# A DiT block with 32 experts on one core: the experts' weights loaded in pieces of 2 MB instead of 1 MB

## The chip, the core and the metric

The kernel runs on one core of one Trainium2 chip. The metric is the device time of one execution in microseconds (us). The core has a matrix engine (TensorE, PE in the profile; PEld is its weight load), a vector engine (DVE), a scalar engine (ACT), GpSimd (POOL) and a sync engine (SP) that here only issues transfers. Sixteen DMA engines move the data between the memory outside (HBM) and the on-chip memory, which has 128 partitions.

## What is computed

One transformer block over 256 tokens of width 1024: modulation from a condition vector, two kinds of attention (global, and windowed with a sink), a gated merge, and then a mixture of 32 experts of which each token uses four. The part that matters here is the mixture; everything is float32.

```python
def moe(h, w_router, b_router, w_e1, b_e1, w_e2, b_e2):
    t = h.reshape(-1, shape[-1])                      # 256 x 1024
    top_logit, top_idx = lax.top_k(t @ w_router + b_router, TOP_K)
    combine = ...                                     # 256 x 32, four weights in a row
    for e in range(N_EXPERTS):                        # 32
        u = t @ w_e1[e] + b_e1[e]                     # w_e1[e]: 1024 x 2048, 8 MB
        u_glu = jnp.minimum(u[:, 0::2], SWIGLU_LIMIT)
        u_lin = jnp.clip(u[:, 1::2], -SWIGLU_LIMIT, SWIGLU_LIMIT)
        act = u_glu * jax.nn.sigmoid(SWIGLU_ALPHA * u_glu) * (u_lin + 1)
        out = out + combine[:, e:e + 1] * (act @ w_e2[e] + b_e2[e])   # w_e2[e]: 1024 x 1024, 4 MB
```

## The kernel before

**The weights' stream.** All large weights pass through areas of 16 KB on each partition (2 MB in all): seven that exist from the start (`ring0` to `ring6`), and two more, `xx` and `ptt`, which the attention uses first and which `grow` hands over when it is done. Each area counts as two halves of 8 KB. The list `pieces` holds every load in order: the modulation's and the projections' weights, `w_br`, `w_o`, and then the experts. `pump` walks it: it takes the oldest free half, issues the piece's transfer on SP (line 111) and stops where no half is free. `done` gives a half back after the last matmul that reads it, and calls `pump`. SP issues strictly in this order; a transfer waits on SP for the engines that last read its half, and for one of eight semaphores that the transfers use in turn (so at most eight of SP's transfers are under way).

**The experts' pieces.** `w1[e, k]` (k = 0 to 7) is one 1 MB piece, 128 rows of the input dimension by 2048 columns; `w2[e, k]` (k = 0 to 3) is 1 MB too, two blocks of 128 rows by 1024. On each partition a piece is one row of 8 KB. The order is: all of w1(0), and then for each e: w1(e+1, 0 and 1), w2(e, 0 to 3), w1(e+1, 2 to 7). The last expert (31) is loaded in halves of its columns: each of its pieces is two transfers of 512 KB whose rows on a partition are pairs of 2 KB (lines 99 and 105).

**The engines' order.** The text of the kernel is the order. Each expert handles up to 64 gathered tokens. For each e: `scatter` adds an earlier pair's result, `bias1(e+1)` starts the sums, `gemm1` (line 835) runs k = 0 of expert e+1, `act_turn(e)` turns expert e's activations, `gemm1` runs k = 1, `gemm2(e)` (line 871) reads the four w2 pieces, `gemm1` runs k = 2 to 7, and `act(e+1)` follows on DVE and ACT. Between two k's there stands now and then a `gather` (line 805) or a `spread` (line 822). A k of `gemm1` is eight PE instructions, a `gemm2` is 32. After expert 30's `gemm1` comes the end: `half1` (line 970) and `half2` (line 1107) of expert 31, with a branch on a register in between (line 1017, a path for overfull experts that isn't taken here).

Of the kernel before, what the change touches and what calls it, by code (L numbers as in the profile page):

```python
# [17 lines left out]
NE = 32  # L18
# [16 lines left out]
def tile_dit_block(ctx: ExitStack, tc: tile.TileContext, xcT, consts, small, rows,  # L35
                   w_m0, w_q, w_mod, w_in, w_br, w_o, w_r, w1, b1, w2, b2, out):
    nc = tc.nc
# [6 lines left out]
    pieces = []  # L44
# [7 lines left out]
    def w1s(e, ks):  # L52
        pieces.extend(("w1", (e, k), w1[e, k]) for k in ks)

    def w2s(e):
        pieces.extend(("w2", (e, k), w2[e, k]) for k in range(4))

    for j in range(10):
        if j < 8:
# [6 lines left out]
    ins(7), mods(10, 11), ins(8), mods(12, 13), ins(9), mods(14, 15)  # L66
    pieces.extend(("br", i, w_br[i]) for i in range(4))
    pieces.extend(("wo", i, w_o[i]) for i in range(4))
    w1s(0, range(8))
    for e in range(NE - 1):  # L70
        w1s(e + 1, range(2))
        w2s(e)
        w1s(e + 1, range(2, 8))
    w2s(NE - 1)


    areas = [per.tile([128, 4096], F32, name=f"ring{i}") for i in range(N_PAIR)]
    spare = [(i, h) for i in range(N_PAIR) for h in range(2)]
    n_next = [0]
    held, place = {}, {}  # L80

    def half(a):
        return areas[a[0]][:, 2048 * a[1]:2048 * a[1] + 2048]

    def pump():
        while n_next[0] < len(pieces):
            kind, idx, src = pieces[n_next[0]]
            if kind == "xc":
                nc.sync.dma_start(out=xc, in_=xcT[1])
                n_next[0] += 1  # L90
                continue
            if not spare:
                return
            place[kind, idx] = spare.pop(0)
            t = held[kind, idx] = half(place[kind, idx])
            if kind == "w2" and idx[0] == NE - 1:
                h, q = divmod(idx[1], 2)
                for b in range(2):
                    nc.sync.dma_start(
                        out=t[:, 1024 * b:1024 * b + 1024].rearrange("p (k c) -> p k c", k=2),  # L100
                        in_=w2[NE - 1, q + 2 * b].rearrange("p (k c) -> p k c", k=2)[:, :, 512 * h:512 * h + 512])
            elif kind == "w1" and idx[0] == NE - 1:
                h, q = divmod(idx[1], 4)
                for b in range(2):
                    nc.sync.dma_start(
                        out=t[:, 1024 * b:1024 * b + 1024].rearrange("p (a c) -> p a c", a=2),
                        in_=w1[NE - 1, 2 * q + b].rearrange("p (a h c) -> p a h c", a=2, h=2)[:, :, h, :])
            elif kind == "q":
                nc.sync.dma_start(out=t[:, 0:1024], in_=src)
            else:  # L110
                nc.sync.dma_start(out=t, in_=src)
            n_next[0] += 1

    def take(kind, idx):
        return held[kind, idx]

    def done(kind, idx):
        held.pop((kind, idx))
        spare.append(place.pop((kind, idx)))
        pump()  # L120

    def grow(t):

        areas.append(t)
        spare.extend((len(areas) - 1, h) for h in range(2))
        pump()
# [153 lines left out]
    for j in range(8):  # L280
# [15 lines left out]
        if j > 4:  # L296
            i, k = ((0, 1), (2, 3), (0, 2))[j - 5]
# [396 lines left out]
    for m in range(8):  # L694
        w = take("wo", m // 2)[:, 1024 * (m % 2):1024 * (m % 2) + 1024].rearrange("p (k c) -> p k c", k=8)
# [133 lines left out]
    def gemm1(e, u, ks, between=None):  # L829
        p, j = divmod(e, 2)  # L830
        for k in ks:
            w = take("w1", (e, k))
            for ch in (0, 2, 1, 3):
                c0 = 64 * (ch // 2)
                nc.tensor.matmul(u[c0:c0 + 64, ch % 2, :], XT[p][:, k, 64 * j:64 * j + 64],  # L835
                                 w[:, 512 * ch:512 * ch + 512], start=False, stop=(k == 7))
            done("w1", (e, k))
            if between and k in between:
                between[k]()

# [13 lines left out]
    def act_turn(e, aT=None):  # L854
        t = TMP.pop(e)
        tp = ps2.tile([128, 4, 128], F32, name="ta", tag="tp")
        for b in range(4):
            nc.tensor.transpose(tp[:, b, :], t[:, 0, 128 * b:128 * b + 128], ident)  # L858
        if aT is None:
            aT = t[:, 3, :].rearrange("p (b s) -> p b s", b=4)  # L860
        nc.scalar.copy(out=aT, in_=tp)  # L861
        return aT

    def gemm2(e, aT, between=None):
        p, j = divmod(e, 2)
        y = ps2.tile([128, 512], F32, name="y", tag="y")
        for k in range(8):
            w = take("w2", (e, k // 2)).rearrange("p (k c) -> p k c", k=2)[:, k % 2, :]
            l = aT[:, k % 4, 64 * (k // 4):64 * (k // 4) + 64]
            for h in range(2):  # L870
                nc.tensor.matmul(y[64 * h:64 * h + 64, :], l, w[:, 512 * h:512 * h + 512],  # L871
                                 start=(k == 0), stop=(k == 7))
            if k % 2:
                done("w2", (e, k // 2))
                if between and k // 2 in between:
                    between[k // 2]()
        if e >= NE - 2:
            YY[e] = x_t[:, 0, 512 * (e % 2):512 * (e % 2) + 512]
            nc.vector.tensor_tensor(out=YY[e], in0=y, in1=g2x, op=ALU.mult)
            return  # L880
        if j == 0:
            YY[p] = y_t[0][:, p % 2, :]
        for h in range(2):
            nc.vector.tensor_tensor(out=YY[p][64 * j:64 * j + 64, 512 * h:512 * h + 512],  # L884
                                    in0=y[64 * h:64 * h + 64, :],
                                    in1=g2[64 * h:64 * h + 64, 512 * h:512 * h + 512], op=ALU.mult)
# [63 lines left out]
    for e in range(NE - 2):  # L950
        p, j = divmod(e, 2)
# [4 lines left out]
        aT = act_turn(e)  # L956
# [5 lines left out]
    e0, e1 = NE - 2, NE - 1  # L962
    sums = {}

    def half1(h, q, u):
        w = take("w1", (e1, 4 * h + q)).rearrange("p (b a c) -> p b a c", b=2, a=2)
        for b in range(2):
            k = 2 * q + b
            for i in range(2):
                nc.tensor.matmul(u[64 * i:64 * i + 64, h, :], XT[e1 // 2][:, k, 64:128], w[:, b, i, :],  # L970
                                 start=False, stop=(k == 7))
        done("w1", (e1, 4 * h + q))

    def act_half(h, u):
        t, c = tmp4, slice(256 * h, 256 * h + 256)
# [23 lines left out]
    aT = act_turn(e0)  # L999
# [17 lines left out]
    with tc.If(cnt > CAP):  # L1017
# [20 lines left out]
        def body(e):  # L1038
            ws = []
            for k in range(8):  # L1040
                w = slots[k]
                nc.sync.dma_start(out=w, in_=w1[bass.ds(e, 1), k].rearrange("e p n -> (e p) n"))
                ws.append(w)
            cv = moe.tile([128, 2], F32, name="cv")
            for tb in range(2):
# [4 lines left out]
            for tb in range(2):  # L1050
                aT = y_t[0][:, tb, :].rearrange("p (k s) -> p k s", k=8)
                for ch in range(4):
# [4 lines left out]
                    t = tmp4  # L1057
                    ub, a = t[:, 0, :], t[:, 1, :]
# [13 lines left out]
            vs = []  # L1072
            for k in range(4):
                w = slots[k]
                nc.sync.dma_start(out=w, in_=w2[bass.ds(e, 1), k].rearrange("e p n -> (e p) n"))
                vs.append(w.rearrange("p (k c) -> p k c", k=2))
            for tb in range(2):
                aT = y_t[0][:, tb, :].rearrange("p (k s) -> p k s", k=8)
                for h in range(2):
                    s = slice(512 * h, 512 * h + 512)  # L1080
# [3 lines left out]
                    t = per.tile([128, 512], F32, name="bt", tag="msb")  # L1084
# [14 lines left out]
    aT = tmp4[:, 3, :].rearrange("p (b s) -> p b s", b=4)  # L1099
    yl = [ps2.tile([128, 512], F32, name="yl", tag="y")]  # L1100

    def half2(h, q):
        w = take("w2", (e1, 2 * h + q)).rearrange("p (k c) -> p k c", k=4)
# [11 lines left out]
    for h in range(2):  # L1115
        s = slice(512 * h, 512 * h + 512)
# [4 lines left out]
        for tb in range(2):  # L1121
            a = ACC[0][:, tb, s]
# [10 lines left out]
    for tb in range(2):  # L1133
# [5 lines left out]
        for h in (1, 0):  # L1139
            s = slice(512 * h, 512 * h + 512)  # L1140
# [25 lines left out]
def _pack(a):  # L1166
    import numpy as np
    f = lambda n: np.asarray(a[n])
    h = np.arange(64)
# [12 lines left out]
    rows[0, 0:8] = f("sink")[0]  # L1182
    rows[0, 32:64] = f("b_router")[0]
    rows[0, 1024:2048] = f("final_g")
    pair = lambda w: np.ascontiguousarray(
        w.reshape(w.shape[:-2] + (w.shape[-2] // 256, 2, 128, w.shape[-1])).swapaxes(-3, -2)
    ).reshape(w.shape[:-2] + (w.shape[-2] // 256, 128, 2 * w.shape[-1]))
    tT = lambda t: np.ascontiguousarray(t.T.reshape(8, 128, 256).transpose(1, 0, 2))
    con = np.ascontiguousarray

# [18 lines left out]
                    .reshape(2, 4, 128, 4, 256).transpose(3, 2, 0, 1, 4)).reshape(4, 128, 2048),  # L1209
        "w_o": con(f("w_o")[0].reshape(8, 128, 4, 2, 128).transpose(2, 1, 3, 0, 4)).reshape(4, 128, 2048),  # L1210
        "w_r": con(f("w_router")[0].reshape(8, 128, 32).transpose(1, 0, 2)),
        "w1": con(f("w_e1")[0].reshape(32, 1024, 4, 256, 2).swapaxes(-1, -2)).reshape(32, 8, 128, 2048),
        "b1": con(f("b_e1")[0].reshape(32, 4, 256, 2).swapaxes(-1, -2)).reshape(128, 512),
        "w2": pair(f("w_e2")[0]),
        "b2": be2,
    }

# [17 lines left out]
```

## Time and profile before

| | us |
|---|---|
| median of 3 runs | 1224.25 (1223.93 to 1226.63) |
| profiled execution, its own time | 1224.82 |
| its span, first to last instruction | 1223.0 |
| PE busy in the span | 1159.1 |
| bytes on SP's and ACT's hardware queues | 454.06 MB + 2.06 MB |

The profile gives for each engine the busy time, and cuts the span into 40 slices of 30.6 us. Matmuls are pipelined and their ends are modelled: a PE that is shown as busy is not a PE at its peak. The front, up to some 275 us, holds the modulation, the attention and the routing; the experts run from there to 1191 us, and the rest is the end of expert 31 and the output.

### The profile page before, as it was taken

The numbers are of one execution on the slowest core, as the hardware profiler recorded it, in microseconds if no ns is written. First come the engines' busy times: TensorE is split into PE (matmuls) and PEld (weight loads), VectorE is DVE, ScalarE is ACT, GpSimd is POOL, SyncE is SP. The second block draws the span as 40 slices with busy tenths as digits, with TensorE's granted clock in tenths as the row PEclk, the third lists the DMA queues.
The fourth block names the chain that finished last, engine by engine and source line by source line (L and its number), as shares of the span: only waits on it lengthen the run. The fifth ranks groups of instructions, "written<-read, shape, count | busy, mean of one in ns | idle before, by whom it ended". The sixth has DMA issues, their size and how long they took to land. (4 is left out here: it accounts for less than half of the span.)

```text
span 1223.0 us, 13639 instructions
## 1 busy us (share of the span) xinstructions
PE 1159.1 (95%) x5624; PEld 529.7 (43%) x5624; DVE 359.1 (29%) x765; ACT 138.8 (11%) x304; POOL 35.2 (3%) x29
## 2 busy tenths in 40 slices
PE   7999999999999999999999999999999899999987
PEld 5888666883343334343434323232323232323222
DVE  3263665332222242322222222222222222222212
ACT  2122553030000000000000000000000000000002
POOL 0231100000000000000000000000000000000000
PEclk9999999999999999999999999999999999999997
DMA  9976655838999999999999999999999999999992
GB/s 379 377 296 212 235 206 201 342 134 361 422 421 421 421 420 421 421 421 421 421 421 422 421 421 421 421 421 421 421 421 421 420 421 421 421 421 421 414 391 75
DMA packets 70066, 458.36 MB, mean 375 GB/s; under 512 B 7848, under 2 KB 8240, under 8 KB 16752
## 3 DMA queue, kind: packets, MB, share of 16 engines
q1 hardware_dynamic: 68304, 454.06, 90.9%
q10 hardware_dynamic: 1296, 2.06, 0.5%
q0 software_dynamic: 400, 1.32, 0.3%
q8 instruction: 46, 0.75, 0.2%
q14 instruction: 20, 0.16, 0.0%
HBM read 456.36 MB, written 1.05 MB: 374 GB/s over the span
## 5 line engine op out<-in xcount | busy, mean ns | idle before, releaser
L835 PE MATMUL u<-ring,t 128*64 128x512 f32 x1488 | 346.0, 600 | 21.7 <-DMA ring<-w 21.7
L835 PEld LDWEIGHTS u<-ring,t 128*64 128x64 f32 x1488 | 99.5, 137 | 223.8 <-issue 162.9
L871 PE MATMUL y<-ring,r_q 128*64 128x512 f32 x832 | 184.2, 593 | 0.0
L884 DVE TENSOR_TENSOR t<-y,r_kv 64x512 f32<-64x512 f32 x60 | 41.3, 689 | 325.6 <-PE y L871 325.2
L871 PEld LDWEIGHTS y<-ring,r_q 128*64 128x64 f32 x832 | 59.3, 137 | 119.6 <-issue 115.8
L845 DVE TENSOR_SCALAR r_q<-u 128x512 f32<-128x512 f32 x31 | 21.4, 692 | 244.0 <-PE u L835 244.0
L835 PE MATMUL u<-ptt,t 128*64 128x512 f32 x320 | 75.6, 598 | 4.4 <-DMA ptt<-w 4.4
L847 ACT ACTIVATE r_q<-r_q 128x512 f32<-128x512 f32 x31 | 19.5, 630 | 505.8 <-DVE r_q L845 505.8
L688 PE MATMUL u<-mtx,keep 128*64 128x512 f32 x256 | 62.2, 604 | 3.0 <-DVE r_q L848 3.0
L805 PEld LDWEIGHTS xg<-mtx,r_y 128*128 128x128 f32 x512 | 58.4, 192 | 12.2 <-issue 12.2
L805 PE MATMUL xg<-mtx,r_y 128*128 128x128 f32 x512 | 61.3, 278 | 0.0
L368 PE MATMUL mm<-xx,ring 128*128 128x256 f32 x256 | 59.9, 385 | 0.0
L894 PE MATMUL sp<-t,mtx 128*128 128x512 f32 x120 | 59.7, 620 | 0.0
L368 PEld LDWEIGHTS mm<-xx,ring 128*128 128x128 f32 x256 | 47.3, 190 | 12.6 <-issue 5.0
L807 DVE TENSOR_TENSOR t<-xg,modb 128x512 f32<-128x512 f32 x32 | 22.1, 692 | 91.1 <-PE xg L805 91.1
L835 PE MATMUL u<-xx,t 128*64 128x512 f32 x176 | 40.4, 596 | 3.7 <-DMA xx<-w 3.7
L835 PEld LDWEIGHTS u<-ptt,t 128*64 128x64 f32 x320 | 21.6, 136 | 48.3 <-issue 34.4
L895 DVE TENSOR_TENSOR r_t<-r_t,sp 128x512 f32<-128x512 f32 x60 | 38.4, 681 | 5.1 <-PE sp L894 5.1
L894 PEld LDWEIGHTS sp<-t,mtx 128*128 128x128 f32 x120 | 20.5, 191 | 39.5 <-issue 39.5
L871 PE MATMUL y<-xx,r_q 128*64 128x512 f32 x160 | 36.3, 594 | 0.0
L688 PEld LDWEIGHTS u<-mtx,keep 128*64 128x64 f32 x256 | 16.3, 135 | 44.6 <-issue 22.6
L861 ACT COPY r_q<-ta 128x512 f32<-128x512 f32 x31 | 18.1, 585 | 145.5 <-PE ta L858 145.5
(245 smaller groups left out, 894.7 us busy)
## 6 DMA issues: line engine op xcount, KB each, us to landing
ring<-w SPq DMA_DIRECT2D x290, 1024.0 KB, 19.8
xx<-w SPq DMA_DIRECT2D x42, 1024.0 KB, 19.8
ptt<-w SPq DMA_DIRECT2D x40, 1024.0 KB, 19.8
ring<-w_mod SPq DMA_DIRECT2D x16, 1024.0 KB, 6.8
ring<-w_in SPq DMA_DIRECT2D x10, 1024.0 KB, 8.7
ring<-w SPq DMA_DIRECT2D x20, 512.0 KB, 11.8
ring<-w_m SPq DMA_DIRECT2D x8, 1024.0 KB, 12.5
ring<-w_q SPq DMA_DIRECT2D x8, 512.0 KB, 12.3
```

The lines of the kernel that those rows point to most:

```text
L368: nc.tensor.matmul(gp[0][:, 0:256], w[:, k, :], x[:, k, :], start=(k == 0), stop=(k == 7))
L688: nc.tensor.matmul(u[c0:c0 + 64, ch % 2, :], ident[:, 4 * e + ch:4 * e + ch + 1].to_broadcast([128, 64]), be1, start=True, stop=False)
L805: nc.tensor.matmul(xp[:, b, :], z[:, tb, 128 * k:128 * k + 128], S[:, tb, :], start=(tb == 0), stop=(tb == 1))
L807: nc.vector.tensor_tensor(out=XT[p][:, 4 * h:4 * h + 4, :], in0=xp, in1=sh2[:, 4 * h:4 * h + 4].unsqueeze(2).to_broadcast([128, 4, 128]), ...
L835: nc.tensor.matmul(u[c0:c0 + 64, ch % 2, :], XT[p][:, k, 64 * j:64 * j + 64], w[:, 512 * ch:512 * ch + 512], start=False, stop=(k == 7))
L845: nc.vector.tensor_scalar(out=glu.rearrange("p (b f) -> p b f", b=2), in0=v[:, :, 0, :], scalar1=LIMIT, scalar2=None, op0=ALU.min)
L847: nc.scalar.activation(out=sg, in_=glu, func=AF.Sigmoid, scale=ALPHA)
L861: nc.scalar.copy(out=aT, in_=tp)
L871: nc.tensor.matmul(y[64 * h:64 * h + 64, :], l, w[:, 512 * h:512 * h + 512], start=(k == 0), stop=(k == 7))
L884: nc.vector.tensor_tensor(out=YY[p][64 * j:64 * j + 64, 512 * h:512 * h + 512], in0=y[64 * h:64 * h + 64, :], in1=g2[64 * h:64 * h + 64, 5 ...
L894: nc.tensor.matmul(sp, t[:, tb, :], y[:, s], start=True, stop=True)
L895: nc.vector.tensor_tensor(out=ACC[0][:, tb, s], in0=ACC[0][:, tb, s], in1=sp, op=ALU.add)
```

## The change

The experts' weights are laid out differently in HBM. `w1` becomes 32 x 4 pieces of 2 MB, each of two k's, and `w2` 32 x 2 pieces of 2 MB, each of four blocks; on each partition a piece is one row of 16 KB, and goes into one whole area. `pump` waits for an area whose two halves are both free; `gemm1` gives the area back after every second k, and `gemm2` after its fourth and its eighth block. The order of the bytes is kept: w1(0), then w1(e+1, first piece), w2(e), w1(e+1, the other three). Pieces ahead of the experts stay at 8 KB, as does the last expert (kinds `l1` and `l2`, with the same transfers of 512 KB and rows of 2 KB); where such a piece needs a half, it takes one of an area already half in use if there is one. The path that isn't taken reads the new layout.

```diff
     def w2s(e):
-        pieces.extend(("w2", (e, k), w2[e, k]) for k in range(4))
+        pieces.extend(("w2", (e, k), w2[e, k]) for k in range(2))
...
-    w1s(0, range(8))
-    for e in range(NE - 1):
-        w1s(e + 1, range(2))
+    w1s(0, range(4))
+    for e in range(NE - 2):
+        w1s(e + 1, (0,))
         w2s(e)
-        w1s(e + 1, range(2, 8))
-    w2s(NE - 1)
+        w1s(e + 1, range(1, 4))
+    halves1()
+    at = len(pieces) - 6
+    pieces[at:at] = [("w2", (NE - 2, k), w2[NE - 2, k]) for k in range(2)]
+    halves2()
...
-            if not spare:
-                return
-            place[kind, idx] = spare.pop(0)
-            t = held[kind, idx] = half(place[kind, idx])
...
+            if kind in ("w1", "w2"):
+                whole = [i for i, h in spare if h and (i, 0) in spare]
+                if not whole:
+                    return
+                i = whole[0]
+                spare.remove((i, 0))
+                spare.remove((i, 1))
+                place[kind, idx] = [(i, 0), (i, 1)]
+                t = areas[i]
+            else:
+                if not spare:
+                    return
+                single = [s for s in spare if (s[0], 1 - s[1]) not in spare]
+                s = (single or spare)[0]
+                spare.remove(s)
+                place[kind, idx] = [s]
+                t = half(s)
...
-            w = take("w1", (e, k))
+            w = take("w1", (e, k // 2))[:, 2048 * (k % 2):2048 * (k % 2) + 2048]
...
-            done("w1", (e, k))
+            if k % 2:
+                done("w1", (e, k // 2))
...
-            w = take("w2", (e, k // 2)).rearrange("p (k c) -> p k c", k=2)[:, k % 2, :]
+            w = take("w2", (e, k // 4)).rearrange("p (k c) -> p k c", k=4)[:, k % 4, :]
...
-            if k % 2:
-                done("w2", (e, k // 2))
...
+            if k % 4 == 3:
+                done("w2", (e, k // 4))
...
-        "w1": con(f("w_e1")[0].reshape(32, 1024, 4, 256, 2).swapaxes(-1, -2)).reshape(32, 8, 128, 2048),
+        "w1": con(f("w_e1")[0].reshape(32, 1024, 4, 256, 2).swapaxes(-1, -2).reshape(32, 4, 2, 128, 2048)
+                  .swapaxes(2, 3)).reshape(32, 4, 128, 4096),
...
-        "w2": pair(f("w_e2")[0]),
+        "w2": con(f("w_e2")[0].reshape(32, 2, 4, 128, 1024).swapaxes(2, 3)).reshape(32, 2, 128, 4096),
```

SP's queue just behind the last `w_o` piece, before the change (a row is line, operation, target <- source, size on 128 partitions, and what SP waits for; DMAHW0 to 7 are the eight semaphores):

```order
L111 DMA ring5_67<-w_o 128x2048 [waits DMAHW1_49,PE_49]
L111 DMA ring2_64<-w1 128x2048 [waits DMAHW2_49,DVE_49,Activation_49]
L111 DMA ring3_65<-w1 128x2048 [waits DMAHW3_49,DVE_49]
L111 DMA ring6_68<-w1 128x2048 [waits DMAHW4_49,DVE_49,Activation_49]
L111 DMA ring5_67<-w1 128x2048 [waits DMAHW5_49,PE_49]
L111 DMA ring4_66<-w1 128x2048 [waits DMAHW6_49,DVE_49,Activation_49]
L111 DMA ring1_63<-w1 128x2048 [waits DMAHW7_49,DVE_49]
L111 DMA xx_69<-w1 128x2048 [waits DMAHW0_49]
L111 DMA xx_69<-w1 128x2048 [waits DMAHW1_49,PE_49]
L111 DMA ptt_70<-w1 128x2048 [waits DMAHW3_49]
L111 DMA ptt_70<-w1 128x2048 [waits DVE_49,DMAHW7_49,PE_49,Activation_49]
L111 DMA ring6_68<-w2 128x2048 [waits DMAHW0_49,PE_49]
```

The same place after the change:

```order
L136 DMA ring5_67<-w_o 128x2048 [waits DMAHW1_49,PE_49]
L136 DMA xx_69<-w1 128x4096 [waits DMAHW2_49,PE_49,Activation_49]
L136 DMA ptt_70<-w1 128x4096 [waits DVE_49,DMAHW3_49,PE_49,Activation_49]
L136 DMA ring6_68<-w1 128x4096 [waits DMAHW0_49,PE_49]
L136 DMA ring0_62<-w1 128x4096 [waits DMAHW4_49,DMAHW1_49,PE_49]
L136 DMA ring3_65<-w1 128x4096 [waits DMAHW5_49,DMAHW2_49,PE_49]
L136 DMA ring1_63<-w2 128x4096 [waits DMAHW6_49,DMAHW3_49,PE_49]
L136 DMA ring2_64<-w2 128x4096 [waits DMAHW7_49,DMAHW4_49,PE_49]
L136 DMA ring4_66<-w1 128x4096 [waits DMAHW5_49,PE_49]
L136 DMA ring5_67<-w1 128x4096 [waits DMAHW6_49,PE_49]
L136 DMA xx_69<-w1 128x4096 [waits DMAHW7_49,PE_49]
```

The first expert's pieces went into single halves as these came free; now `xx` and `ptt` come first, and each ring area is loaded once its second half is free. The last of the nine areas, `ring5`, waits for the last `w_o` piece in both.

PE's order at the end of expert 30's `gemm1`, the last expert before the pieces of 512 KB (target `u`, the piece's area, and the wait for its transfer), before the change:

```order
L835 MATMUL u_4740<-ring1_63,t80_75 64x512 [waits DMAHW3_49]
L835 MATMUL u_4740<-ring1_63,t80_75 64x512 x3
L835 MATMUL u_4740<-xx_69,t80_75 64x512 [waits DMAHW4_49]
L835 MATMUL u_4740<-xx_69,t80_75 64x512 x3
L835 MATMUL u_4740<-xx_69,t80_75 64x512 [waits DMAHW5_49]
L835 MATMUL u_4740<-xx_69,t80_75 64x512 x3
L894 MATMUL sp_4836<-t81_76,mtx_1349 128x512
```

The same place after the change:

```order
L860 MATMUL u_4554<-ring6_68,t80_75 64x512 [waits DMAHW4_49]
L860 MATMUL u_4554<-ring6_68,t80_75 64x512 x3
L847 MATMUL tq_4625<-keep_103,SW_4620 128x128 [waits DVE_49,PE_49]
L847 MATMUL tq_4625<-keep_103,SW_4620 128x128 [waits DVE_49]
L860 MATMUL u_4554<-ring6_68,t80_75 64x512 x4
L860 MATMUL u_4554<-ring0_62,t80_75 64x512 [waits DMAHW5_49]
L860 MATMUL u_4554<-ring0_62,t80_75 64x512 x7
L918 MATMUL sp_4650<-t81_76,mtx_1341 128x512
```

PE's matmuls stand in the same order; the waits moved, from one for every k to one for every two, so that k = 6 and k = 7 of expert 30 now wait for one transfer.

## Rows read from the trace of the kernel before

**Rows 1.** Page: rate in 40 slices of the span, and all DMA packets by size

```profile
GB/s 379 377 296 212 235 206 201 342 134 361 422 421 421 421 420 421 421 421 421 421 421 422 421 421 421 421 421 421 421 421 421 420 421 421 421 421 421 414 391 75
DMA packets 70066, 458.36 MB, mean 375 GB/s; under 512 B 7848, under 2 KB 8240, under 8 KB 16752
```

**Rows 2.** Page, transfers: target, queue, count, KB each, us from issue to landing

```profile
ring<-w SPq DMA_DIRECT2D x290, 1024.0 KB, 19.8
xx<-w SPq DMA_DIRECT2D x42, 1024.0 KB, 19.8
ptt<-w SPq DMA_DIRECT2D x40, 1024.0 KB, 19.8
ring<-w SPq DMA_DIRECT2D x20, 512.0 KB, 11.8
```

**Rows 3.** SP's waits, 720 to 1130 us: us in total, times, longest

```profile
SPq L111 <- DMA ring<-w: 270.2, 128, 3.3
...
SPq L111 <- PE u L835: 3.2, 12, 0.4
```

**Rows 4.** Stretches: length, busy us by engine, PE's granted clock, DMA share, GB/s

```profile
9.00:33.00 24.00, 23.01 (x170) 17.30 (x170) 7.89 (x23) 3.42 (x9) 1.64 (x2) 1.00 1.02 419
300.00:690.00 390.00, 386.82 (x1816) 144.80 (x1814) 101.02 (x189) 19.61 (x35) 0.72 (x3) 1.00 1.01 421
740.00:1130.00 390.00, 366.39 (x1693) 130.52 (x1692) 88.84 (x167) 17.86 (x32) 0.00 (x0) 1.00 1.01 421
1176.00:1190.00 14.00, 9.11 (x38) 2.62 (x32) 2.50 (x8) 1.16 (x3) 0.00 (x0) 0.98 1.05 386
```

**Rows 5.** ACT's timeline: start us, us; once an expert; two experts apart in each pair

```profile
516.08 0.63 ACT L847 ACTIVATE r_q<-r_q 128x512 f32<-128x512 f32 x1 [7.44 <-DVE r_q L845]
...
570.77 0.63 ACT L847 ACTIVATE r_q<-r_q 128x512 f32<-128x512 f32 x1 [7.44 <-DVE r_q L845]
...
1039.88 0.63 ACT L847 ACTIVATE r_q<-r_q 128x512 f32<-128x512 f32 x1 [10.20 <-DVE r_q L845]
...
1099.47 0.63 ACT L847 ACTIVATE r_q<-r_q 128x512 f32<-128x512 f32 x1 [9.94 <-DVE r_q L845]
```

**Rows 6.** SP's timeline: the last load into a free area, the first into a released one

```profile
265.44 0.33 SPq L111 DMA_DIRECT2D ring<-w  x1
...
277.48 0.33 SPq L111 DMA_DIRECT2D ring<-w  x1
```

**Rows 7.** Stretches between those two and after them, columns as in rows 4

```profile
273.00:278.00 5.00, 5.00 (x36) 3.30 (x36) 3.01 (x14) 1.69 (x3) 0.00 (x0) 1.00 0.00 0
278.00:285.00 7.00, 7.00 (x34) 2.27 (x32) 0.93 (x5) 0.37 (x1) 0.00 (x0) 1.00 0.90 321
```

**Rows 8.** PE's timeline at the first experts: start us, us, line, count

```profile
275.51 7.09 PE L835 MATMUL u<-ring,t 128*64 128x512 f32 x32
282.52 0.44 PE L822 MATMUL tq<-keep,SW 128*128 128x128 f32 x2
...
291.46 1.94 PE L688 MATMUL u<-mtx,keep 128*64 128x512 f32 x8 [1.48 <-DVE r_q L848]
...
295.64 1.94 PE L835 MATMUL u<-ptt,t 128*64 128x512 f32 x8
```

**Rows 9.** PE's timeline from expert 30's last piece to the branch

```profile
1153.82 1.94 PE L835 MATMUL u<-xx,t 128*64 128x512 f32 x8 [0.54 <-DMA xx<-w]
1156.33 1.94 PE L835 MATMUL u<-xx,t 128*64 128x512 f32 x8 [0.57 <-DMA xx<-w]
1158.19 1.98 PE L894 MATMUL sp<-t,mtx 128*128 128x512 f32 x4
...
1184.55 1.94 PE L970 MATMUL u<-ring,t 128*64 128x512 f32 x8
1191.20 3.68 PE L970 MATMUL u<-ring,t 128*64 128x512 f32 x8 [4.71 <-PEq L1017]
```

**Rows 10.** Stretches around two of PE's idle times, columns as in rows 4

```profile
290.00:292.00 2.00, 0.54 (x4) 0.32 (x6) 1.88 (x3) 0.63 (x1) 0.00 (x0) 1.00 1.00 422
...
1190.00:1192.00 2.00, 0.80 (x2) 0.33 (x4) 0.00 (x0) 0.00 (x0) 0.00 (x0) 0.50 1.03 379
```

More of the change, by code (lines that the diff above doesn't have):

```diff
@@ L55, in w2s, with halves1, halves2 @@
     def w2s(e):
-        pieces.extend(("w2", (e, k), w2[e, k]) for k in range(4))
+        pieces.extend(("w2", (e, k), w2[e, k]) for k in range(2))
+    def halves1():
+        pieces.extend(("l1", q, None) for q in range(8))
+    def halves2():
+        pieces.extend(("l2", q, None) for q in range(4))
     for j in range(10):
@@ L91, in pump @@
                 continue
-            if not spare:
-                return
-            place[kind, idx] = spare.pop(0)
-            t = held[kind, idx] = half(place[kind, idx])
-            if kind == "w2" and idx[0] == NE - 1:
-                h, q = divmod(idx[1], 2)
+            if kind in ("w1", "w2"):
[15 more added lines that the diff above has]
+                t = half(s)
+            held[kind, idx] = t
+            if kind == "l2":
+                h, q = divmod(idx, 2)
                 for b in range(2):
@@ L100, in pump @@
                         out=t[:, 1024 * b:1024 * b + 1024].rearrange("p (k c) -> p k c", k=2),
-                        in_=w2[NE - 1, q + 2 * b].rearrange("p (k c) -> p k c", k=2)[:, :, 512 * h:512 * h + 512])
-            elif kind == "w1" and idx[0] == NE - 1:
-                h, q = divmod(idx[1], 4)
+                        in_=w2[NE - 1, b].rearrange("p (q k c) -> p q k c", q=2, k=2)[:, q, :, 512 * h:512 * h + 512])
+            elif kind == "l1":
+                h, q = divmod(idx, 4)
                 for b in range(2):
@@ L106, in pump @@
                         out=t[:, 1024 * b:1024 * b + 1024].rearrange("p (a c) -> p a c", a=2),
-                        in_=w1[NE - 1, 2 * q + b].rearrange("p (a h c) -> p a h c", a=2, h=2)[:, :, h, :])
+                        in_=w1[NE - 1, q].rearrange("p (b a h c) -> p b a h c", b=2, a=2, h=2)[:, b, :, h, :])
             elif kind == "q":
@@ L118, in done @@
         held.pop((kind, idx))
-        spare.append(place.pop((kind, idx)))
+        spare.extend(place.pop((kind, idx)))
         pump()
@@ L862, in act_turn, with gemm2 @@
         return aT
-    def gemm2(e, aT, between=None):
+    def gemm2(e, aT):
         p, j = divmod(e, 2)
@@ L872, in gemm2 @@
                                  start=(k == 0), stop=(k == 7))
-            if k % 2:
-                done("w2", (e, k // 2))
-                if between and k // 2 in between:
-                    between[k // 2]()
+            if k % 4 == 3:
+                done("w2", (e, k // 4))
         if e >= NE - 2:
@@ L965, in half1 @@
     def half1(h, q, u):
-        w = take("w1", (e1, 4 * h + q)).rearrange("p (b a c) -> p b a c", b=2, a=2)
+        w = take("l1", 4 * h + q).rearrange("p (b a c) -> p b a c", b=2, a=2)
         for b in range(2):
@@ L971, in half1 @@
                                  start=False, stop=(k == 7))
-        done("w1", (e1, 4 * h + q))
+        done("l1", 4 * h + q)
     def act_half(h, u):
@@ L1041, in body @@
                 w = slots[k]
-                nc.sync.dma_start(out=w, in_=w1[bass.ds(e, 1), k].rearrange("e p n -> (e p) n"))
+                nc.sync.dma_start(
+                    out=w, in_=w1[bass.ds(e, 1), k // 2].rearrange("e p n -> (e p) n")[:, 2048 * (k % 2):2048 * (k % 2) + 2048])
                 ws.append(w)
@@ L1074, in body @@
                 w = slots[k]
-                nc.sync.dma_start(out=w, in_=w2[bass.ds(e, 1), k].rearrange("e p n -> (e p) n"))
+                nc.sync.dma_start(
+                    out=w, in_=w2[bass.ds(e, 1), k // 2].rearrange("e p n -> (e p) n")[:, 2048 * (k % 2):2048 * (k % 2) + 2048])
                 vs.append(w.rearrange("p (k c) -> p k c", k=2))
@@ L1102, in half2 @@
     def half2(h, q):
-        w = take("w2", (e1, 2 * h + q)).rearrange("p (k c) -> p k c", k=4)
+        w = take("l2", 2 * h + q).rearrange("p (k c) -> p k c", k=4)
         for b in range(4):
@@ L1184, in _pack @@
     rows[0, 1024:2048] = f("final_g")
-    pair = lambda w: np.ascontiguousarray(
-        w.reshape(w.shape[:-2] + (w.shape[-2] // 256, 2, 128, w.shape[-1])).swapaxes(-3, -2)
-    ).reshape(w.shape[:-2] + (w.shape[-2] // 256, 128, 2 * w.shape[-1]))
     tT = lambda t: np.ascontiguousarray(t.T.reshape(8, 128, 256).transpose(1, 0, 2))
```

## The prediction

> **What bounds the kernel now.** I read the rates by slice first. From the tenth slice on DMA moves 420 to 422 GB/s, flat, until the last slices [rows 1]; ahead of that it swings between 134 and 379. The experts are therefore fed at a constant rate. Then I asked whether that rate or PE sets the pace. Between 516 and 571 us a pair of experts takes 54.69 us; between 1040 and 1099 it takes 59.59 [rows 5]. The first is PE's own pace, while it still eats what was loaded ahead: 27.3 us an expert. The second is the stream's: 12 pieces of 1.0486 MB at 421 GB/s are 29.9 us [rows 4]. So PE catches up with the stream and then waits for pieces, some 0.55 us each [rows 9], and the stream sets the end. SP agrees: from 720 to 1130 us it waits 270.2 us for ring transfers to land and hardly for PE (3.2 us) [rows 3]: eight transfers are always under way, and a landing takes 19.8 us, eight times 2.5 [rows 2].
>
> Where does that hold? At the start, DMA has filled all nine areas (18 MB) with the load issued at 265.44; the next goes out at 277.48, when PE has used the first piece [rows 6], and between 273 and 278 nothing moves [rows 7]. At the end, the last wait of PE for a transfer is that for expert 30's last piece, at 1156.33; the twelve groups from there to 1184.55 bear none, and then the branch holds PE until 1191.20 [rows 9]. So the path is: front to 277, stream to 1156, then PE to the end.
>
> **The change: rate.** What does a packet cost? The page counts 70,066 packets, of which 53,314 have 8 KB or more [rows 1]; the 416 transfers of 1 MB with 128 rows each (372 of them experts' pieces [rows 2]) make 53,248, so a row of 8 KB travels as one packet. With 16 engines at 421 GB/s one takes 16 x 8192 B / 421 = 311.3 ns of its engine. In the stretch with nothing but rows of 2 KB (the last expert) the rate is 386 [rows 4], or 84.9 ns a packet. Each engine also moves one small packet per transfer (the 7,848 under 512 B are about 16 for each of some 460 transfers): one per 8 rows of 8 KB, one per 16 rows of 2 KB. With c per byte and o per packet of either kind, 8192c + 1.125 o = 311.3 and 2048c + 1.0625 o = 84.9, so o = 9.05 ns and 8192c = 301.1 ns (435 GB/s without o). Is it per packet or per transfer? If all of it hung on the transfer, 512 KB transfers would run at 386 whatever their rows. From 9 to 33 us a third of the bytes comes in 512 KB transfers with rows of 4 KB; per packet I get 409 GB/s for those and 417 for the mix, per transfer 409 for the mix; the row says 419 [rows 4]. So per packet. A row of 16 KB should then take 602.2 + 10.2 = 612.4 ns instead of 2 x 311.3 = 622.6: 428 GB/s, 1.64% less time. No row shows a packet of 16 KB. The estimate extends a line of three sizes by one doubling; its ends by rounding of 421 and 386 (half a GB/s each) are 1.59 and 1.68%. If the row is cut in two on the way, only the small packets halve: 0.57 of 311.3 ns, 0.18%.
>
> How many bytes gain? To the end of expert 30's w1 there are 31 x 8 + 30 x 4 = 368 pieces of 1 MB; 18 lie in the areas before 277, in both kernels. 350 x 1.0486 MB / 421 = 871.7 us, of which 1.64% is **14.3 us** (13.9 to 14.6).
>
> The page "SBUF — State Buffer" of the Trainium skill (section "The DMA setup-cost knee") puts a fixed 2 us on every transfer, which fewer transfers would save. Charged to the stream, 175 fewer transfers would give 350 us. The trace disagrees: 1 MB every 2.5 us at 421 GB/s leaves no 2 us free, since eight are under way at once.
>
> **The change: coarser pieces.** Three places can pay.
> At the start, the first area is free after k = 1, not k = 0. A k takes 1.77 us (7.09 for four) [rows 8], so the first load goes out at 279.2 instead of 277.5: **+1.7 us** on the stream. It may be less: from 278 to 285 the stream ran at only 321 [rows 7], since it then got 1 MB at a time; the 1.7 us lost there may come back in part, so 0.8 to 1.7. Next could be a gap: a 2 MB load lasts 4.9 us. With releases at 279.2, 282.7, 286.4, 289.9 and, after the activation's wait, 297.4 (the end of the group at 295.64) [rows 8], four loads last to some 300; the fifth is out 2 us or more ahead. Gap 0, at most 1.
> At the end, k = 6 and 7 of expert 30 both wait for the last piece; before, only k = 7 did: **+1.8 us** (0 if PE lags there anyway).
> In between, PE waits longer for each piece (4.9 us against 3.5 of work, up to 1.4 us), but the stream is the bound and pays nothing. SP's in-order queue now holds 2 MB loads behind PE's releases; what stands behind them is only the next load, and with nine areas seven or eight remain issued. In the front, the same pieces go to the same halves; the first expert's loads now queue behind `xx` and `ptt`, but all nine areas still are filled once the last w_o piece is released at 265 [rows 6], and 2 MB land by about 271. Cost 0; if a load were missing at 275, its whole landing time would show.
> The end from 1158 on has the same matmuls, and its 512 KB loads come at the same rate. PE starts there 1.8 us later against the stream, so data are if anything earlier.
>
> Sum for the profiled execution: 1224.82 - 14.3 + 1.7 + 1.8 = 1214.0. The median of the runs is 0.57 lower than that execution, so **1213.4 us**.
>
> **Rivals.**
> *A ceiling in between.* The 16 engines may have a limit of their own below 428; the longest stretches show 421 [rows 4]. With half of the gain it is 1224.25 - 7.2 + 3.5 = 1220.6. The line through three sizes speaks against it, the jump beyond them for it. The page "HBM Reference" of the Trainium skill (section "Specifications (TRN2)") gives about 425 GB/s for a core alone, bounded by its 16 DMA engines. By that figure the gain is 0.94% or 8.2 us and the time 1219.5; no stretch of rows 4 reaches it.
> *The row is cut in two* (the change doesn't do what it says on the engines): -1.6 + 3.5 gives 1226.2, within 0.2%.
> *Slower by rate.* Long rows may be read worse, as 16 engines then step through HBM 16 KB apart. Each per cent of rate is 8.7 us; at 1% under today's, 1224.25 + 8.7 + 3.5 = 1236.5. It decides from where the gain is under 0.12%, because of the 3.5 us. For it: nothing measured at 16 KB. Against: from 2 to 8 KB the rate only rises.
> *Slower by clock.* PE's granted clock is 0.50 at 1190, after 4.7 us idle, and 1.00 at 290 to 292, around 1.48 us idle [rows 8 to 10]. The waits of up to 1.4 us are nearer to the second. If it fell in every pair, eight matmuls would take 3.68 instead of 1.94 for a while [rows 9], and the pair's 4 us of slack would be gone: above 1230.
> *The branch.* PE's 4.71 us at L1017 and the half clock behind it may move or vanish as the waits in front of it change: up to some 9 us less, 1204.
>
> **How the numbers follow.** Forecast 1213.4: 0.62, with a range of its own of 1212 to 1216. Ceiling 0.12, cut row 0.10, slower by rate 0.07, slower by clock 0.03, branch 0.06. About 0.2% (2.45 us) is what a measurement of this kernel can tell from no change. Faster: 0.62 + 0.12 + 0.06 = 0.80; same 0.10; slower 0.10. The range runs from 1210 (below the forecast's low end, for part of the branch) to 1227 (the cut row), leaving out 0.16.
>
> **What would show it.** Rate in the expert stretch 427 to 429 GB/s; 16 KB packets, so some 26,800 packets fewer in all (23,808 of data and 2,976 small ones); 58.8 us a pair late in the stream; first release near 279.2; PE's waits fewer and longer; the end from expert 30's last piece on unchanged in length but for 1.8 us. Wrong if the rate stays within 1 GB/s of 421, if DMA's share drops between 279 and 320, if a clock below 1.00 stands between 300 and 1150 for long, or if the branch's wait differs from 4.7 us.

## The result, and the profile after the change

The changed kernel takes 1210.21 us (median of 4 runs, 1209.79 to 1211.22) against 1224.09 before (4 runs, 1221.46 to 1226.63): a ratio of 0.9891, interval 0.9871 to 0.9910. A second series gave 1210.69 against 1221.98, 0.9908 (0.9892 to 0.9924). The profiled execution took 1209.79 us, its span 1208.0. One of the six runs of experiment 5 below was a slow one (1336.76 us, mean granted clock 0.85) and is left out of its median.

The page first: the rate by slice, all packets, and the transfers of the weights. They answer to [rows 1, 2].

```profile
GB/s 379 385 301 213 240 175 53 352 296 335 427 428 428 427 427 428 427 427 428 427 429 427 428 428 425 430 427 427 429 426 426 428 428 428 429 426 429 417 396 89
DMA packets 43279, 458.32 MB, mean 379 GB/s; under 512 B 4872, under 2 KB 5264, under 8 KB 13776
...
ring<-w SPq DMA_DIRECT2D x144, 2048.0 KB, 32.2
xx<-w SPq DMA_DIRECT2D x21, 2048.0 KB, 32.4
ptt<-w SPq DMA_DIRECT2D x21, 2048.0 KB, 29.7
```

The expert slices show 425 to 430 where they showed 420 to 422, and the packets are 26,787 fewer; the prediction's count was 23,808 + 2,976 = 26,784. So a row of 16 KB does travel as one packet. How exact is the rate? The view of the DMA queues between 330 and 1120 us, first of before, then of after (packets, MB, share of 16 engines), leaves out the edges:

```profile
q1 hardware_dynamic: 45607, 332.14, 101.1%
```

```profile
q1 hardware_dynamic: 23153, 337.24, 100.4%
```

Over 790 us that is 420.4 and 426.9 GB/s, 1.51% less time for a byte. The stretches of the prediction, columns as in [rows 4, 7]:

```profile
273.00:278.00 5.00, 5.00 (x31) 2.55 (x31) 3.58 (x17) 0.53 (x2) 0.00 (x0) 1.00 0.04 15
278.00:285.00 7.00, 7.00 (x34) 2.26 (x32) 0.00 (x0) 0.37 (x1) 0.00 (x0) 1.00 0.88 323
...
300.00:690.00 390.00, 386.82 (x1816) 144.72 (x1814) 100.96 (x189) 19.61 (x35) 0.72 (x3) 1.00 1.01 428
740.00:1130.00 390.00, 367.63 (x1722) 135.68 (x1723) 89.11 (x166) 18.61 (x33) 0.00 (x0) 1.00 1.01 427
```

PE still catches up and then waits. A late pair of experts takes 58.72 us on ACT's timeline, where [rows 5] had 59.59:

```profile
1030.33 0.63 ACT L873 ACTIVATE r_q<-r_q 128x512 f32<-128x512 f32 x1 [9.86 <-DVE r_q L871]
...
1089.05 0.63 ACT L873 ACTIVATE r_q<-r_q 128x512 f32<-128x512 f32 x1 [9.84 <-DVE r_q L871]
```

SP's waits from 720 to 1130 us (total, times, longest), against [rows 3]: most are still for landings, but SP now waits for PE as well, since an area must be free as a whole. The rate shows no cost of it: it holds at 427, as other 2 MB loads are under way meanwhile.

```profile
SPq L136 <- DMA ring<-w: 235.4, 60, 6.1
SPq L136 <- PE u L860: 46.5, 20, 8.6
```

At both ends of the stream the timelines look as follows. SP's first load into a released area ([rows 6]), then PE at the first experts ([rows 8]):

```profile
278.02 0.33 SPq L136 DMA_DIRECT2D xx<-w  x1
```

```profile
274.33 3.65 PE L860 MATMUL u<-xx,t 128*64 128x512 f32 x16
277.81 3.60 PE L860 MATMUL u<-ptt,t 128*64 128x512 f32 x16
```

and PE from expert 30's last two pieces to the branch ([rows 9]):

```profile
1138.40 1.94 PE L860 MATMUL u<-ring,t 128*64 128x512 f32 x8 [1.25 <-DMA ring<-w]
1140.27 0.44 PE L847 MATMUL tq<-keep,SW 128*128 128x128 f32 x2
1140.63 1.94 PE L860 MATMUL u<-ring,t 128*64 128x512 f32 x8
1143.34 3.65 PE L860 MATMUL u<-ring,t 128*64 128x512 f32 x16 [0.77 <-DMA ring<-w]
1146.92 1.99 PE L918 MATMUL sp<-t,mtx 128*128 128x512 f32 x4
...
1179.90 3.10 PE L994 MATMUL u<-xx,t 128*64 128x512 f32 x8 [4.70 <-PEq L1041]
1182.93 2.47 PE L1017 MATMUL sp<-t,mtx 64*128 64x512 f32 x4
1185.34 1.94 PE L994 MATMUL u<-xx,t 128*64 128x512 f32 x8
```

These starts cut both spans at the same five points, so the difference can be booked by place:

| stretch (us) | before | after | difference |
|---|---|---|---|
| start to expert 0's first gemm1 | 275.51 | 274.33 | -1.18 |
| to the first load into a released area | 1.97 | 3.69 | +1.72 |
| to the matmuls on expert 30's last piece | 878.85 | 865.32 | -13.53 |
| to the scatter `sp` behind expert 30 | 1.86 | 3.58 | +1.72 |
| to the first matmul behind the branch | 33.01 | 32.98 | -0.03 |
| to the end of the span | 31.80 | 28.10 | -3.70 |

The middle three are the change, -10.09 us. The first is not: a second profiled execution of the same changed kernel reached expert 0 at 275.40. The last is the subject of experiments 5 and 6. Below, "the stream's stretch" is the sum of the middle three, from expert 0's first gemm1 to the scatter behind expert 30: 882.68 us before, 872.59 after (872.49 in the second execution). It isn't the same in every execution: the kernels without the branch (experiments 5, 6 and 11), which are the same as these up to there, show 881.85 for before and 872.71 and 872.89 for after. So the change is worth 9.0 to 10.2 us of it.

### The profile page after: what moved, and what is told of

Its sections match the earlier page's. It is cut to its first block, busy times and chain, and to the rows that moved or that the text cites. A ratio compares the mean times of both kernels' runs of the same rounds, so it can differ in the third digit from the quotient of the medians.

```text
span 1208.0 us, 13270 instructions
## 1 busy us (share of the span) xinstructions
PE 1147.9 (95%) x5624; PEld 531.5 (44%) x5624; DVE 360.0 (30%) x765; ACT 138.8 (11%) x304; POOL 35.1 (3%) x29
## 5 line engine op out<-in xcount | busy, mean ns | idle before, releaser
L860 PE MATMUL u<-ring,t 128*64 128x512 f32 x1472 | 337.3, 599 | 19.6 <-DMA ring<-w 19.2
L860 PE MATMUL u<-ptt,t 128*64 128x512 f32 x336 | 78.2, 597 | 2.5 <-DMA ptt<-w 2.2
## 6 DMA issues: line engine op xcount, KB each, us to landing
ring<-w SPq DMA_DIRECT2D x144, 2048.0 KB, 32.2
xx<-w SPq DMA_DIRECT2D x21, 2048.0 KB, 32.4
```

## The experiments

**1 and 2. Size, place and row apart.** The first keeps all that the change does but the layout in HBM: 2 MB transfers, each of two rows of 8 KB on a partition.

```diff
-        pieces.extend(("w1", (e, k), w1[e, k]) for k in ks)
+        pieces.extend(("w1", (e, k), w1[e, 2 * k:2 * k + 2]) for k in ks)
...
+            elif kind in ("w1", "w2"):
+                nc.sync.dma_start(out=t.rearrange("p (b n) -> p b n", b=2), in_=src.rearrange("b p n -> p b n"))
```

> The changed kernel, but each transfer of 2 MB moves two rows of 8 KB per partition (the weights lie in HBM as in the kernel before). Areas, order, releases and the number of transfers are those of the changed kernel. If the cost hangs on the packet, the rate in the expert stretch is 422 GB/s (16 data packets of 8 KB and one small one per engine and transfer), some 23,800 packets more than after the change, a pair late in the stream takes 59.6 us, and the time is 12 to 13 us above the changed kernel's 1210.2: 1222 to 1224. If it is the size of the transfer, whatever its rows, the rate is 427 to 428 and the time 1210 to 1212.

The second keeps the areas and the order, but loads each area by two transfers of 1 MB.

```diff
+            elif kind in ("w1", "w2"):
+                for b in range(2):
+                    nc.sync.dma_start(out=t[:, 2048 * b:2048 * b + 2048], in_=src[b])
```

> The changed kernel's areas, order and releases, but every piece of 2 MB comes as two transfers of 1 MB with rows of 8 KB, as before the change. What is left of the change is the coarser release and wait and the new places of the first expert. My sum: the rate is 421, the first release 1.7 us later and expert 30's last wait 1.8 us dearer: 1 to 3.5 us above the kernel before, 1225 to 1228 against 1224.1. If the coarse pieces are hidden: equal to the kernel before, 1224. If the new places or the releases bring a gain of their own: below 1222.

Measured: 1227.37 us for 2 MB with 8 KB rows, 1.0023 of before (1.0009 to 1.0038); 1220.96 us for two times 1 MB, 0.9988 (0.9975 to 1.0001). Neither has the gain. The first lies above the 1222 to 1224 that were expected: its stretch is 13.2 us longer than the changed kernel's, about as expected, but in the profiled execution its end behind the branch is 4.1 us longer too (32.2 us against 28.1). The second lies below the 1222 that would have meant a gain by the new places, but before took 1222.67 beside it and the interval reaches 1.0001. The queue of the first between 330 and 1120 us:

```profile
q1 hardware_dynamic: 43097, 332.28, 101.0%
```

That is 420.6 GB/s: transfers of twice the size at the rate of before. Only the row of 16 KB brings 426.9. The second didn't test all that I meant it to: its first load goes out 1.98 us after the first gemm1 starts, and PE waits 0.55 and 0.58 us for expert 30's last pieces, as before, so each 1 MB is waited for by itself. It shows that new places and order cost nothing that can be told. The first then has the price of the coarse ends alone. Its stream's stretch is 885.76 us:

```profile
275.33 3.65 PE L862 MATMUL u<-xx,t 128*64 128x512 f32 x16
...
1161.09 1.98 PE L920 MATMUL sp<-t,mtx 128*128 128x512 f32 x4
```

Against 882.68 before, 882.49 in the second and 881.85 in experiment 5 these are **3.1 to 3.9 us**, from one execution.

**3 and 4. Where the coarse pieces cost.** The changed kernel with 1 MB pieces at the two ends (first area given back in halves, expert 30's k = 6 and 7 apart), and at the last end alone. The edit of the latter, in the list and in `gemm1`:

```diff
+    FINE = (NE - 2,)
...
+        if e + 1 in FINE:
+            w1s(e + 1, range(1, 3))
+            h1s(e + 1, (6, 7))
...
+            if e in FINE and k > 5:
+                w = take("h1", (e, k))
```

> The changed kernel, but at both ends of the stream the pieces are 1 MB again: the first area is given back in halves (after k = 0 and after k = 1 of expert 0) and refilled with two 1 MB pieces, and expert 30's last 2 MB come as two transfers of 1 MB. If my two terms are right (+1.7 at the start, of which 0.8 to 1.7 tell, and +1.8 at the end), this is 2.6 to 3.5 us faster than the changed kernel: 1206.7 to 1207.6. If the coarse pieces are hidden at both ends: 1210.

> The changed kernel, with 1 MB pieces only at the end of the stream (expert 30's last 2 MB). If the last wait costs its 1.8 us: 1208.4. If it is hidden: 1210. The difference to the run with both ends is what the first release costs: 0.8 to 1.7 by my sum.

Measured: 1212.07 us (ratio to before 0.9917, 0.9899 to 0.9936) and 1213.14 (0.9925, 0.9906 to 0.9944); no gain over the changed kernel's 0.9908. The stretches are 871.49 and 871.70 us, against 872.5 to 872.9 in four executions of the changed kernel: 1.0 to 1.4 and 0.8 to 1.2 us came back, not 3. Why so little at the end? PE's timeline of the kernel with the fine last end:

```profile
1139.40 1.94 PE L871 MATMUL u<-ring,t 128*64 128x512 f32 x8 [1.26 <-DMA ring<-w]
1141.27 0.44 PE L855 MATMUL tq<-keep,SW 128*128 128x128 f32 x2
1141.64 5.37 PE L871 MATMUL u<-ring,t 128*64 128x512 f32 x24
1146.94 1.98 PE L931 MATMUL sp<-t,mtx 128*128 128x512 f32 x4
```

The wait for the last piece is gone, and from the 1.26 us wait for the 2 MB of k = 4 and 5 on PE works without a stop. That piece now sets the end. At the start, the rate dips from 9 to 12.5 us after the first gemm1 (columns as in [rows 4]):

```profile
283.41:286.91 3.50, 3.50 (x18) 1.15 (x16) 0.00 (x0) 0.00 (x0) 0.00 (x0) 1.00 0.95 332
```

In the changed kernel the same stretch shows 426. The first two halves leave earlier, but the second area is still given back whole, 7.1 us after the first gemm1, and its load is too late to fill that stretch. At both ends, then, the next piece inward is as coarse; that this is the reason is tested in experiments 8 to 11.

**5 and 6. The end behind the branch.** The kernel before and the changed one, both without the branch and its path.

```diff
-    cnt = nc.values_load(cint[0:1, 0:1], min_val=0, max_val=256)
-    with tc.If(cnt > CAP):
...
```

> The changed kernel once more, beside the runs below. The stretch behind the branch ran 3.7 us shorter in its profiled execution than in that of the kernel before (28.1 against 31.8 us), because the clock stood at 0.50 for a shorter time. If that belongs to the change, it is 28 again and the median 1210; if it varies from run to run, the stretch lies anywhere from 27 to 32 us and the times spread with it.

> The kernel before without the branch on a register (the path for overfull experts is left out, which isn't taken here). PE then has no 4.7 us of waiting at that place and no half clock behind it: 4.7 + 5 us less, but not earlier than the last expert's data allow: 1214 to 1217. The clock stays at 1.00 from 1150 us on. Difference to the changed kernel without the branch: 11.3 us if the clock's return is what made the end shorter, 14 to 15 if the change itself shortens the end.

> The changed kernel without the branch on a register. 4.7 us less and the rest of the half clock, some 2 us: 1202 to 1205. Difference to the kernel before without the branch: 11.3 us if only stream, first release and last wait differ; 14 to 15 if the change shortens the end as well.

Measured, on one chip: changed kernel 1210.69 us, before without branch 1213.22 (0.9930 of before, 0.9912 to 0.9947), changed without branch 1203.70 (0.9848, 0.9831 to 0.9866). Without the branch the change is worth 9.5 us; with it 11.3 to 13.9. So neither of the expected differences came: the 11.3 held the 1.18 us ahead of the experts, which aren't the change's, and the stretches of these two executions differ by 9.1 us (881.85 and 872.71), not 10.1. From the scatter behind expert 30 to the end both now take the same, 54.35 and 54.39 us. So the rest sits behind the branch. The clock there in before, stretch by stretch:

```profile
1192.00:1196.00 4.00, 4.00 (x10) 1.20 (x7) 0.00 (x0) 0.00 (x0) 0.00 (x0) 0.50 0.66 247
1196.00:1200.00 4.00, 4.00 (x8) 1.02 (x8) 0.00 (x0) 0.00 (x0) 0.00 (x0) 0.50 0.25 96
1200.00:1202.00 2.00, 2.00 (x8) 0.49 (x6) 0.00 (x0) 0.00 (x0) 0.00 (x0) 0.50 0.00 0
```

and in after:

```profile
1180.00:1184.00 4.00, 4.00 (x10) 1.13 (x11) 0.00 (x0) 0.00 (x0) 0.00 (x0) 0.57 0.57 216
1184.00:1186.00 2.00, 2.00 (x8) 0.67 (x8) 0.00 (x0) 0.00 (x0) 0.00 (x0) 1.00 0.16 56
```

After the same idle time (4.71 and 4.70 us) the granted clock stays at 0.50 (1.2 GHz) for some 12 us in one and for some 4 in the other. It isn't the change that chooses: over the nine profiled executions with the branch the time from the first matmul behind it to the end is 31.8, 32.2, 32.1 and 32.4 us (before, experiments 1, 4 and 9) or 28.1, 28.7, 27.9, 28.6 and 28.0 (after, its second execution, experiments 2, 3 and 8). Both lengths occur with 8 KB rows (32 us before and in experiment 1, 28 in experiment 2) and with 16 KB rows. What decides between them stays open.

**7. The rate by itself.** A kernel that only loads, ten stretches of 33.5 MB each, with the transfer's size, the row's length and the number of queues changed (here the loads of three stretches: 1 MB with rows of 8 KB, 2 MB with rows of 8 KB, 2 MB with rows of 16 KB; the numbers are words of 4 bytes on a partition):

```diff
+    for i in range(32):
+        nc.sync.dma_start(**ends(2048, 2048, i))
+    for i in range(16):
+        nc.sync.dma_start(**ends(4096, 2048, i))
+    for i in range(16):
+        nc.sync.dma_start(**ends(4096, 4096, i))
```

> No block at all: only loads of 33.5 MB each in ten stretches, without any reader, then an output of loaded words. Per packet o = 9.05 ns and 301.1 ns per 8 KB give: 1 MB with rows of 2 KB 387 GB/s; 512 KB with rows of 4 KB 409; 1 MB with rows of 4 KB 410; 1 MB with rows of 8 KB 421; 2 MB with rows of 8 KB 422; 2 MB with rows of 16 KB 428; 4 MB with rows of 16 KB 428.4; 4 MB with rows of 32 KB 431.6. If the size of the transfer counts and not the row, 2 KB, 4 KB and 8 KB at 1 MB are alike, and the two kinds at 2 MB and at 4 MB too. The last two stretches (1 MB with 8 KB, 2 MB with 16 KB, issued in turn on SP and ACT): as with one queue if the engines' work per packet sets the rate, up to 435 if a second queue hides it.

Measured, one row out of the middle of each stretch (length, POOL busy, clock, DMA share, GB/s); in order: 1 MB with rows of 2 KB; 512 KB, 4 KB; 1 MB, 4 KB; 1 MB, 8 KB; 2 MB, 8 KB; 2 MB, 16 KB; 4 MB, 16 KB; 4 MB, 32 KB; and issued by SP and ACT in turn 1 MB, 8 KB and 2 MB, 16 KB:

```profile
20.00:75.00 55.00, 0.00 (x0) 1.00 1.05 387
100.00:155.00 55.00, 0.00 (x0) 1.00 1.03 410
190.00:235.00 45.00, 0.00 (x0) 1.00 1.03 410
265.00:315.00 50.00, 0.00 (x0) 1.00 1.01 422
345.00:390.00 45.00, 0.00 (x0) 1.00 1.01 422
...
412.00:484.00 72.00, 0.00 (x0) 1.00 1.01 429
490.00:560.00 70.00, 0.00 (x0) 1.00 1.01 428
570.00:620.00 50.00, 0.00 (x0) 1.00 1.01 434
...
660.00:700.00 40.00, 0.00 (x0) 1.00 1.01 422
725.00:790.00 65.00, 0.00 (x0) 1.00 1.01 428
```

Twice the transfer with the same row changes nothing, three times over (410 and 410, 422 and 422, 429 and 428); twice the row brings 23, 12, 7 and, by the last step's windows, 6 GB/s (3 by a steadier measure, given at the end); a second issuing queue brings nothing. Up to 16 KB every forecast is met within 1 GB/s.

**8 to 11. Both ends finer still.** If the next piece inward was the reason why experiments 3 and 4 got so little back, it must go too: expert 30's k = 4 to 7 as 1 MB (8); the same, and the first two areas given back in halves (9); that without the branch (10), beside experiment 6's kernel again (11). The edit of (9), against experiment 3; in (8) it is `k > 3` in experiment 4's lines:

```diff
-    FINE = (1, NE - 2)
+    FINE = {1: (6, 7), 2: (0, 1), NE - 2: (4, 5, 6, 7)}
...
-            if (e, k) == (0, 0):
+            if (e, k) in ((0, 0), (0, 2)):
```

> The changed kernel, with expert 30's w1 from k = 4 on as four pieces of 1 MB. In e4_fine_end, where only k = 6 and 7 came so, the stretch from expert 0's first gemm1 to the scatter behind expert 30's gemm1 was 871.70 us against 872.5 of the changed kernel, and PE had no wait left behind the 1.26 us for the 2 MB of k = 4 and 5. Theory one (that piece then set the end, and the coarse end costs 3.59 - 1.86 = 1.73 us in all): with it cut as well, the stretch is some 870.8 us, and PE again waits some 0.5 us for each of the last pieces. Theory two (a coarse end costs no more than the 0.8 us that came back): 871.7 again.

> The changed kernel with 1 MB pieces at both ends: the first two areas are given back in halves, and refilled with 1 MB pieces (expert 1's k = 6, 7 and expert 2's k = 0, 1), and expert 30's k = 4 to 7 come as 1 MB. In e3_fine_ends only the first area was, and the rate fell to 332 GB/s between 9.0 and 12.5 us after expert 0's first gemm1 (the second area's 2 MB were asked for 7.1 us after it). Theory one: with the second area in halves that gap closes; the bytes moved in the first 45 us after expert 0's first gemm1 are 17.4 MB or more, against 17.00 in the changed kernel and 17.15 in e3; the stretch to the scatter behind expert 30 is 872.5 - 1.7 - 1.0 = 869.8 us. Theory two (fine ends return 1 us and no more): 871.5. The median time would by theory one be 1208, but the end behind the branch differs by up to 4 us from run to run, so the stretch decides, not the median.

> As e9_fine_all, and the branch with the path for overfull experts is left out (that path isn't taken with this input). Without the branch the end has one length (54.4 us from the scatter behind expert 30), so a gain of 2 us can be seen. Theory one (a coarse start and end cost 3.0 us together, and fine pieces return them): 2.7 us below e11_nobranch_again, 1201.0 us. Theory two: 1.0 us below it, 1202.7.

> The changed kernel without the branch, as in e6_after_nobranch (1203.7 us), beside e10_fine_all_nobranch on one chip. Both theories expect 1203 to 1204.5 us and 54.4 us from the scatter behind expert 30 to the end.

Measured: (8) one time of 1210.7 us, a stretch of 871.16. (9) 1213.85 us (1209.30 to 1215.57; 0.9921 of before, 0.9890 to 0.9951), a stretch of 871.69. (10) 1201.64 us (1201.28 to 1203.14) and 870.45; (11) 1203.88 (1203.39 to 1204.03) and 872.89. Experiment 10's end has the small waits back:

```profile
1139.43 3.71 PE L874 MATMUL u<-ring,t 128*64 128x512 f32 x16
1143.72 1.94 PE L874 MATMUL u<-ring,t 128*64 128x512 f32 x8 [0.58 <-DMA ring<-w]
1145.59 1.98 PE L939 MATMUL sp<-t,mtx 128*128 128x512 f32 x4
```

The dip at the start is gone: 419 and 421 GB/s from 9 to 12.5 us in (9) and (10), where experiment 3 had 332. Between 10 and 11 lie 2.2 us in the median and 2.4 in the stretch, nearer to the 2.7 of theory one than to the 1.0 of theory two. Experiment 9 doesn't agree: its stretch is theory two's 871.5 and not theory one's 869.8. In its first 45 us from expert 0 on the queue moved 17.09 MB, in experiment 10, with the same loads, 17.40. Experiment 8 lies between its two theories. At the start one run differs from the next by as much as is at stake there, so theory one rests on the comparison of 10 and 11. Without the branch the finer ends are thus shown to be faster. With the branch in place nothing of it is seen in the median, behind the 4 us of the clock: no version with the branch is shown to beat the changed kernel.

## Why the prediction was right, and where it wasn't

It was faster, for the forecast's reason, by a little more than forecast: 1210.21 us against 1213.4. The change itself brought a little less than forecast (9.0 to 10.2 us of the stream's stretch, where the prediction's sum was 10.8). That the time is lower all the same, 0.2 us inside the low end of the range, is owed to the 3.7 us behind the branch. The range had left room for them, by a rival with a chance of 0.06, but no run shows that the change brings them, so as far as is known this is luck. With the end of before, the profiled execution would have taken 1213.5 us, and 1214.7 with its front as well, where 1214.0 was forecast for it.

**The rate** held as a mechanism: per packet, not per transfer (experiments 1 and 7), with the packets counted to within three. What in a packet costs the time isn't told apart: no run here changes the length of a row without that of a packet. The term that was mis-sized is the gain by the rate, by some 9%: 1.51% of 871.7 us are 13.2 us, not 14.3, and below the 13.9 that rounding allowed. Measured in the kernel, a pair of 8 KB packets takes 2 x 16 x 8192 B / 420.4 = 623.6 ns of an engine and a packet of 16 KB 614.1: 9.5 ns saved, where 10.2 were expected (one overhead and an eighth). The overhead of 9.05 ns was taken from two rounded rates in two parts of the kernel; whether it is too large stays open, since experiment 7's rates fit it. One step of the working was misread: from 9 to 33 us a quarter of the bytes comes in rows of 4 KB (640 packets of that size, 2.6 of 10.0 MB), not a third. The sums for the mix are then 418 GB/s per packet and 411 per transfer, and the 419 measured still speaks for the packet.

**The ceiling** that the prediction feared didn't show. The page "HBM Reference" of the Trainium skill (section "Specifications (TRN2)") gives about 425 GB/s for a core alone; 427 and 428 in the kernel, 429 and more in experiment 7 say otherwise, and its 1219.5 us didn't come.

**The knee.** The page "SBUF — State Buffer" of the Trainium skill (section "The DMA setup-cost knee") has DMA-bound loads gathered into the largest single transfer. No run here shows a gain by that, with several transfers under way: in experiment 7, 1 MB and 2 MB with rows of 8 KB both move 422 GB/s.

**The first release** came 3.69 us after the first gemm1 instead of 1.97, +1.72 as predicted. Its cost for the stream is 1.3 to 1.9 us: in the first 45 us from the first gemm1 the queue moved 16.70 MB in experiment 1, and 17.25, 17.37 and 17.49 MB before and in experiments 2 and 5, whose first load leaves after 1.97 or 1.98 us, all at the same later rate. The 0.55 to 0.79 MB are 1.3 to 1.9 us at 420.4. So the 1.7 that the prediction took may stand. What doesn't stand is its reason for less than that, that the stream ran thin between 278 and 285 because it got 1 MB at a time: experiment 5 has the same loads at the same places, and runs nearly full there. From 6 to 9 us after the first gemm1, before and in experiment 5:

```profile
281.51:284.51 3.00, 3.00 (x16) 0.97 (x14) 0.00 (x0) 0.37 (x1) 0.00 (x0) 1.00 1.02 363
```

```profile
280.50:283.50 3.00, 3.00 (x16) 0.97 (x14) 0.00 (x0) 0.37 (x1) 0.00 (x0) 1.00 1.00 418
```

What thins it in some executions stays open.

**The last piece** cost 1.72 us, predicted 1.8. What the prediction didn't see is that one finer piece can't undo it: the piece before it is late too (experiments 4 and 8).

**Between the ends** coarse pieces cost nothing, as predicted (420.6 GB/s with 2 MB pieces in experiment 1, 420.4 before); PE's waits became fewer and longer, up to 1.25 us at the end, and the granted clock is 1.00 from 300 to 690 and from 740 to 1130 us. The rival of the clock is out.

The sum by measured terms is -13.2 + 1.3 to 1.9 + 1.7 = -10.2 to -9.6 us, and the stream's stretch says -10.09 in the two profiled executions, -9.0 to -10.2 over all of them. The prediction had -10.8.

**Behind the branch** the prediction counted on an unchanged end, and gave the half clock's length to a rival. The 3.7 us there, which make the time lie below the forecast, come with this clock: without the branch both ends are alike, and with it both lengths occur in kernels with either row. Whether the changed kernel meets the short end more often, or the runs happened to fall so, is open: the ratios of 0.9891 and 0.9908 contain it, and the 9.5 us without the branch are free of it.

## What to carry to other kernels

Where a stream of loads is the bound and several are always under way, look at the length of the row on each partition, not at the size of the transfer: packets per byte set the rate, and the gain of the next doubling can be read from the last ones. A coarser piece was paid for at the two ends of the stream, once each, by what it delays: the first release and the work behind the last landing. To see a gain of 2 us behind a part that differs by 4 us from run to run, measure between two points of the trace, in more than one execution (the same stretch differed here by up to 0.8 us), or take that part out.

## What was not expected of the hardware

- Rows of 32 KB gain little more. The 434 GB/s above depend on where the 50 us are cut: stretches of 10 us in them go from 423 to 442. In that part of experiment 7 each load of 4 MB goes into an area that an earlier one filled, and SP waits for its landing. The last five such loads start 9.72 us apart, 431.6 GB/s, as expected; those with rows of 16 KB start 9.78 us apart, 428.9.
- Counted over all queues, rows of 16 KB reach 427 and 428 GB/s in the kernel and 428 or 429 alone, those of 8 KB 421 and 422. What the last GB/s goes to wasn't tried.
- After an idle time of 4.7 us PE's granted clock is 0.50, and it comes back to 1.00 after some 4 us of matmuls in some executions and some 12 in others, at a cost of 4 us. Leaving the branch out, with that idle time and that clock, made the kernel before 8.8 us faster (1221.98 to 1213.22), nearly as much as the whole change.
